# Moving window unpacking out of a ramp, dropping fillers, and cutting the last block's products into five pieces, in a graph attention kernel

## The chip, the cores and the metric

The kernel runs on one core of a Trainium2 chip. The metric is device time in microseconds (us). The profile's span, from the first to the last instruction, is about 1.8 us shorter than the time of the same run (289.9 against 291.72 for the kernel before). A 2% difference is 5.8 us.

PE is the matmul engine (TensorE) and PEld its weight load, DVE is VectorE, ACT is ScalarE, POOL is GpSimd, SP is SyncE, whose queue issues most transfers. L493 means line 493 of the kernel in question; the change shifts lines after 540 by a few.

## The reference

It is a graph attention layer on 4096 nodes with 64 features, 4 heads of 64, and 50,000 random edges:

```python
x_proj[h] = x @ weight[h]
score[h, e] = leaky_relu(x_proj[h, src] . att_src[h] + x_proj[h, dst] . att_dst[h], 0.2)
output[h, dst] += exp(score[h, e]) * x_proj[h, src]          # over all edges e
output[h, dst] /= sum of exp(score[h, e]) over edges into dst, + 1e-8
# result: 4096 x 256, f32
```

## The kernel before

It sorts the edges by destination (to about 112 us). Then it works on 33 blocks of 125 destination nodes; a block's edges are 16 tiles of 128. For each block the SP queue loads a table `bc` of 1 MB (edge keys, repeated on all partitions). VectorE turns it into one-hot matrices `oh`, TensorE gathers features and scores with them, ScalarE makes exponentials `ex` and copies `xs`, VectorE picks the leaky maximum (`wv`) and multiplies (`val`), and TensorE sums `val` into destinations and projects.

The tables come from `gat_bins` in HBM, which is filled by five "unpacks". Each serves eight blocks: window `i` serves blocks 8i to 8i+7.

```python
def unpack(self, i):                                   # Windows
    t, tb = self.t[:, i], self.tb[:, i]
    V.tensor_scalar(out=t[:, 1, :], in0=self.win[:, i, :], ..., op0=OP.bitwise_and)          # L441
    V.tensor_scalar(out=t[:, 0, :], in0=self.win[:, i, :], ..., op0=OP.logical_shift_right)  # L442
    e = G if i else V
    e.tensor_copy(out=tb[:, 1, :], in_=t[:, 1, :])                                           # L445
    e.tensor_scalar(out=tb[:, 0, :], in0=t[:, 0, :], scalar1=boff[:, i:i + 1], ...)          # L446
    nc.sync.dma_start(out=bin_dram[8 * i:8 * i + 8]..., in_=tb)                              # L447
```

`G` is GpSimd, `V` VectorE, `S` ScalarE, `T` TensorE. The `dma_start` on `nc.sync` goes into the same queue as the table loads and the results, and the traces show that queue in the program's order (before: bins at 126.06, block 5's load at 131.75, the first result at 137.60). The ramp, which fills the pipeline for blocks 0 to 2:

```python
busy(11)                       # fillers: matmuls without use, meant to keep TensorE's clock up
win.unpack(0)
for b in range(2, 5):
    blocks.load(b)
blocks.weights(0)
blocks.values(0)               # block 0's product
for c in range(len(CH)):       # block 1's table: made by TensorE ("spread", L479), copied by ScalarE (L481)
    blocks.spread(1, c, ...)
    if c == 1:
        blocks.onehot(1, *CH[0])
... # one-hots of block 1, sums of block 0, gathers of block 1
for i in range(1, NI):         # NI = 5
    win.unpack(i)
blocks.sums(0, 1)
busy(3)
blocks.onehot(2)
blocks.weights(1)
blocks.run(1)
```

And the loop:

```python
def run(self, first=0):
    for b in range(first, ND):
        self.load(b + 4)                               # 1 MB on the SP queue
        self.values(b, 2 if b == ND - 1 else 1)        # the product val
        self.gather(b + 1, 0); self.sink.project(b - 1); self.sums(b, -1)
        self.gather(b + 1, 1); self.gather(b + 1, 2)
        self.sink.invert(b - 1)
        self.onehot(b + 2, halves=(0,))
        self.weights(b + 1)
        self.onehot(b + 2, halves=(1,))
        self.sink.give(b - 1)                          # result, written on the SP queue
        self.sums(b, 0); self.sums(b, 1)
```

(Conditions on `b` and the line breaks are cut.)

## Time and profile before

| | before |
|---|---|
| time, median of 5 | 291.72 us (291.0 to 292.1) |
| span of the profiled run, mean granted clock | 289.9 us, 0.864 |
| busy share PE / DVE / ACT / POOL | 71 / 89 / 66 / 12 % |
| product `val` of blocks 1, 2, 3, 4 starts at | 131.40, 137.50, 142.82, 147.53 us |
| a block step from there on | 4.71 us |
| product of block 31 | 274.79 us |

A block's product occurs once a step, and in the loop the distance between two of them is 4.71 us. Whatever a version gains or loses can be read as a shift of this series, and located between two blocks. Time minus block 31's product is 16.93 us before.

### The profile page before, as it was taken

To read this page: it belongs to the slowest core of one execution; us is meant where nothing else is said; L and a number is where in the kernel's file an instruction comes from. 1 tells how busy PE (TensorE), PEld (TensorE's weight loads), DVE (VectorE), ACT (ScalarE), POOL (GpSimd) and SP (SyncE) were. 2 spreads that over 40 slices of the span, in tenths; PEclk is the share of its full clock that TensorE was granted. 3 is DMA by queue.
4 is the path that set the end of the run, shared out by engine and by line. 5 is a ranking of instruction groups with operands and counts; after the bars stand their busy time and mean duration, and the time that the engine had idled before them with its cause. 6 is when DMAs were issued, how large, how long until landed. Compare 5 with 4: busy or idle time off the path is not lost.

```text
span 289.9 us, 8530 instructions
## 1 busy us (share of the span) xinstructions
PE 205.4 (71%) x3531; PEld 195.1 (67%) x3531; DVE 259.3 (89%) x526; ACT 190.9 (66%) x392; POOL 33.9 (12%) x81
## 2 busy tenths in 40 slices
PE   0011899950000066859999999999999999999990
PEld 0010699950000025549999999999999999999980
DVE  5999999993699999857999999999999999999970
ACT  2960710041699938554888888888888888888860
POOL 7882000002000001751000000000000000000000
PEclk9999975555555559996999999999999999999997
DMA  3026000001100001495576766768586767675011
GB/s 110 0 55 111 0 2 0 0 2 40 33 0 0 0 0 40 174 331 170 202 278 225 276 242 255 263 232 288 211 295 214 293 217 283 224 267 190 23 38 43
DMA packets 12688, 40.77 MB, mean 141 GB/s; under 512 B 1840, under 2 KB 8272, under 8 KB 8672
## 3 DMA queue, kind: packets, MB, share of 16 engines
q1 hardware_dynamic: 10128, 37.91, 35.7%
q10 hardware_dynamic: 1808, 1.56, 2.3%
q0 software_dynamic: 704, 0.66, 1.2%
q8 instruction: 30, 0.49, 0.7%
q14 instruction: 18, 0.15, 0.2%
HBM read 35.08 MB, written 5.05 MB: 138 GB/s over the span
## 4 chain that ended last, share of the span: by engine, by line

## 5 line engine op out<-in xcount | busy, mean ns | idle before, releaser
L524 ACT CAST xs<-ps 128x1200 bf16<-128x1200 f32 (+1 forms) x99 | 104.1, 1052 | 0.0
L542 DVE TENSOR_TENSOR val<-xs,wv 128x4096 bf16<-128x4096 bf16 (+1 forms) x34 | 75.4, 2219 | 0.4 <-ACT xs L524 0.2
L516 PE MATMUL ps<-adb,oh 128*128 128x136 bf16 x528 | 62.7, 225 | 0.0
L514 PE MATMUL ps<-xa,oh 128*128 128x72 bf16 x528 | 59.9, 198 | 3.7 <-DVE oh L493 2.1
L567 PE MATMUL acc<-xs,val 128*128 128x125 bf16 x1024 | 62.0, 219 | 0.0
L567 PEld LDWEIGHTS <-val 128*128 128x128 bf16 x1056 | 58.8, 98 | 0.3 <-DVE val L542 0.3
L516 PEld LDWEIGHTS <-oh 128*128 128x128 bf16 x528 | 49.8, 99 | 1.5 <-issue 1.4
L514 PEld LDWEIGHTS <-oh 128*128 128x128 bf16 x528 | 47.6, 99 | 3.2 <-DVE oh L493 3.2
L281 PE MATMUL cnt_ps<-sgn,sel 128*128 128x17 f32 (+1 forms) x6 | 1.6, 385 | 60.7 <-ACT sgn L273 41.7
L493 DVE TENSOR_SCALAR oh<-bc,pF 128x4096 bf16<-128x4096 bf16 (+2 forms) x37 | 42.6, 1152 | 0.6 <-ACT bc L481 0.6
L281 PEld LDWEIGHTS cnt_ps<-sgn,sel 128*128 128x128 f32 x6 | 1.4, 318 | 60.8 <-issue 60.8
L522 ACT ACTIVATE ex<-ps 128x96 bf16<-128x96 f32 (+1 forms) x99 | 25.0, 252 | 26.2 <-PE ps L520 26.1
L202 DVE TENSOR_TENSOR sA<-sB 128x256 f32<-128x256 f32 (+2 forms) x104 | 37.2, 399 | 1.5
L202 DVE TENSOR_TENSOR sB<-sA 128x256 f32<-128x256 f32 (+2 forms) x98 | 35.1, 399 | 1.3
L520 PE MATMUL ps<-xa,oh 128*128 128x72 bf16 x528 | 33.9, 199 | 0.0
L520 PEld LDWEIGHTS <-oh 128*128 128x128 bf16 x528 | 26.9, 100 | 0.0
L495 DVE TENSOR_SCALAR oh<-bc,pF 128x2048 bf16<-128x2048 bf16 (+2 forms) x37 | 25.6, 691 | 0.0
L420 PEld LDWEIGHTS at_ps<-uv,xT 64*128 64x128 f32 x130 | 24.9, 298 | 0.3 <-issue 0.3
L420 PE MATMUL at_ps<-uv,xT 64*128 64x4 f32 x130 | 25.0, 329 | 0.0
L270 ACT ACTIVATE junk<-kr,nb 128x512 f32<-128x512 f32 x33 | 23.8, 722 | 1.1
L629 PE MATMUL pf<-Wbd,aT 128*128 128x128 f32 (+1 forms) x132 | 23.3, 299 | 0.5 <-ACT aT L621 0.5
L560 PEld LDWEIGHTS <-xs 128*128 128x128 bf16 x528 | 18.7, 96 | 0.4
(141 smaller groups left out, 231.0 us busy)
## 6 DMA issues: line engine op xcount, KB each, us to landing
bc<-gat_bins SPq DMA_DIRECT2D x31, 1024.0 KB, 5.1
out_dram<-res SPq DMA_DIRECT2D x32, 125.0 KB
eD<-in_edge_index_dram ACTq DMA_DIRECT2D x2, 195.0 KB, 3.3
eS<-in_edge_index_dram SPq DMA_DIRECT2D x2, 195.0 KB
gat_bins<-tb SPq DMA_DIRECT2D x5, 64.0 KB, 5.1
gat_sorted<-sA SPq DMA_DIRECT2D x1, 256.0 KB, 2.0
gat_sorted<-ki SPq DMA_DIRECT2D x1, 256.0 KB
win<-gat_sorted,to POOLq DMA_INDIRECT x5, 2.5
```

The source lines that it names most:

```text
L202: V.tensor_tensor(out=av(d[:], o, [2 * h, n], [1, h]), in0=av(s[:], 0, [2 * h, n], [1, h]), in1=av(s[:], h, [2 * h, n], [1, h]), op=op)
L270: S.activation(out=junk[:], in_=v, func=ACTF.Sign, bias=nbnd[:, b:b + 1], scale=1.0, accum_out=sgn[:, b:b + 1])
L420: T.matmul(out=ps[:, b, :], lhsT=xT[:, b * step:b * step + P], rhs=uv[:, k, :], start=(b == 0), stop=True, skip_group_check=True)
L493: V.tensor_scalar(out=oh[:, e], in0=bc[:, e], scalar1=pF[:, 0:1], scalar2=None, op0=OP.is_equal)
L495: V.tensor_scalar(out=av(oh[:], (2 * NT + t0) * W2, [W2, nt], [1, W2]), in0=av(bc[:], (2 * t0 + 1) * W2, [2 * W2, nt], [1, W2]), scalar1=p ...
L514: T.matmul(out=ps[:, i, P:P + XC], lhsT=hot(2 * t + 1), rhs=xa[:, 2 * t, :], start=(i % 2 == 0), stop=False, skip_group_check=True)
L516: T.matmul(out=ps[:, i, 0:S0], lhsT=hot(2 * t), rhs=adb[:, b, :], start=False, stop=False, skip_group_check=True)
L520: T.matmul(out=ps[:, i, P:P + XC], lhsT=hot(2 * NT + t), rhs=xa[:, 2 * t + 1, :], start=False, stop=True, skip_group_check=True)
L522: S.activation(out=av(ex[:], 2 * t0, [2, n], [2 * NT, 2 * H], [1, 2]), in_=av(ps[:], P, [PW, n], [1, 2 * H], [0, 2]), func=ACTF.Exp)
L524: S.copy(out=xs[:, t0:t0 + n, 0:P + XC], in_=ps[:, 0:n, 0:P + XC])
L542: V.tensor_tensor(out=av(val[:], h * Dout, [Dout, n], [C, NT], [1, Din]), in0=av(xs[:], S0, [0, n], [XW, NT], [1, Din]), in1=av(wv[:], h * ...
L567: T.matmul(out=self.to[k], lhsT=val[:, t, k * P:(k + 1) * P], rhs=xs[:, t, 0:self.n], start=apart and t == 0, stop=(t == NT - 1), skip_gro ...
```

## The change

Unpacks 3 and 4 serve blocks 24 to 32, yet VectorE waits for their windows in the ramp. The change moves them to the ends of block steps 1 and 2, drops seven of the ramp's fourteen fillers, and cuts the last block's product so that the second sum of the tail can begin earlier.

```diff
-            for h in range(0, H, n):
-                V.tensor_tensor(out=av(val[:], h * Dout, [Dout, n], [C, NT], [1, Din]), ...)
+            for h, nh, t, n in ((0, 2, 0, NT), (2, 1, 0, 12), (3, 1, 0, 12), (2, 1, 12, 4),
+                                (3, 1, 12, 4)) if parts > 1 else ((0, H, 0, NT),):
+                V.tensor_tensor(out=av(val[:], h * Dout + t * C, [Dout, nh], [C, n], [1, Din]), ...)
...
-        def run(self, first=0):
+        def run(self, first=0, also={}):
...
                 self.sums(b, 0)
                 self.sums(b, 1)
+                if b in also:
+                    also[b]()
...
-            if n != H:
-                m = min(n, 2 * BD)
-                S.copy(out=self.aT[b][:, at:at + m], in_=acc[:, 0:m])
+            elif n != H:
+                part = self.fp.tile([P, n], F32, name=f"part{at}")
+                S.copy(out=part[:], in_=acc)
...
-        busy(11)
+        busy(7)
...
-        for i in range(1, NI):
+        for i in range(1, 3):
             win.unpack(i)
         blocks.sums(0, 1)
-        busy(3)
         blocks.onehot(2)
         blocks.weights(1)
-        blocks.run(1)
+        blocks.run(1, {i - 2: lambda i=i: win.unpack(i) for i in range(3, NI)})
```

(The rest of the diff is bookkeeping for the part tiles.)

More of the change, by code (lines that the diff above doesn't have):

```diff
@@ L539, in values @@
             val = self.bp.tile([P, NT, C], BF16, name="val")
-            n = H // parts
-            for h in range(0, H, n):
-                V.tensor_tensor(out=av(val[:], h * Dout, [Dout, n], [C, NT], [1, Din]),
-                                in0=av(xs[:], S0, [0, n], [XW, NT], [1, Din]),
-                                in1=av(wv[:], h * 2 * NT, [2, n * NT], [0, Din // 2], [1, 2]), op=OP.mult)
+            for h, nh, t, n in ((0, 2, 0, NT), (2, 1, 0, 12), (3, 1, 0, 12), (2, 1, 12, 4),
+                                (3, 1, 12, 4)) if parts > 1 else ((0, H, 0, NT),):
+                V.tensor_tensor(out=av(val[:], h * Dout + t * C, [Dout, nh], [C, n], [1, Din]),
+                                in0=av(xs[:], S0 + t * XW, [0, nh], [XW, n], [1, Din]),
+                                in1=av(wv[:], h * 2 * NT + 2 * t, [2, nh * n], [0, Din // 2], [1, 2]), op=OP.mult)
             self.val[b] = val
@@ L610, in __init__ @@
             self.apart = True
-            self.aT = {}
+            self.aT, self.den = {}, {}
             self.fp = ctx.enter_context(tc.tile_pool(name="fin", bufs=2))
@@ L617, in take @@
             if n in (AW, H):
-                self.aT[b] = self.fp.tile([P, AW], F32, name="aT")
-            if n != H:
-                m = min(n, 2 * BD)
-                S.copy(out=self.aT[b][:, at:at + m], in_=acc[:, 0:m])
+                self.den[b] = self.fp.tile([P, AW], F32, name="aT")
+            t = self.den[b]
+            if n == AW:
+                S.copy(out=t[:, 0:2 * BD], in_=acc[:, 0:2 * BD])
+                self.aT[b] = [t[:, k * BD:k * BD + P] for k in range(2)]
+            elif n != H:
+                part = self.fp.tile([P, n], F32, name=f"part{at}")
+                S.copy(out=part[:], in_=acc)
+                self.aT.setdefault(b, []).append(part[:])
             if n in (AW, H):
-                S.activation(out=self.aT[b][:, 2 * BD:AW], in_=acc[:, n - H:n], func=ACTF.Identity, bias=eps[:, 0:1])
+                S.activation(out=t[:, 2 * BD:AW], in_=acc[:, n - H:n], func=ACTF.Identity, bias=eps[:, 0:1])
         def project(self, b):
             self.pf = self.psf.tile([P, C], F32, name="pf")
-            m = min(P, N - b * BD)
-            for k in range(2):
-                T.matmul(out=self.pf[0:m, k * P:(k + 1) * P], lhsT=self.aT[b][:, k * BD:k * BD + m], rhs=Wbd[:, k, :],
+            for k, t in enumerate(self.aT.pop(b)):
+                T.matmul(out=self.pf[0:t.shape[-1], k * P:(k + 1) * P], lhsT=t, rhs=Wbd[:, k, :],
                          start=(k == 0), stop=True, skip_group_check=True)
@@ L633, in invert @@
             self.inv = self.fp.tile([P, H], F32, name="inv")
-            V.reciprocal(out=self.inv[0:BD], in_=self.aT.pop(b)[0:BD, 2 * BD:AW])
+            V.reciprocal(out=self.inv[0:BD], in_=self.den.pop(b)[0:BD, 2 * BD:AW])
         def give(self, b, parts=1):
```

## The prediction

> **What bounds the kernel now.** I read the page first, then the table by stage, then VectorE's timeline at the two places that the change touches, and the waits there. The kernel is a sort (to about 112 us), a ramp that prepares the first blocks of 125 destination nodes (112 to 143 us), a steady loop over blocks (to 279 us) and a tail. The change touches the ramp and the tail. The table by stage (columns: stretch, its length, busy time of PE, PEld, DVE, ACT, POOL, then granted clock, DMA share, GB/s), cut at the points where the TensorE clock changes:
>
> ```profile
> 122.40:125.80 3.40, 3.40 (x76) 3.40 (x76) 2.88 (x9) 2.21 (x4) 1.09 (x3) 1.00 1.00 345
> 125.80:129.20 3.40, 1.24 (x11) 0.55 (x8) 0.83 (x5) 1.68 (x5) 2.11 (x6) 1.00 0.99 352
> 129.20:132.60 3.40, 2.16 (x21) 2.16 (x22) 3.30 (x4) 0.54 (x2) 2.10 (x2) 0.51 0.47 161
> 132.60:136.00 3.40, 3.40 (x53) 3.34 (x52) 2.35 (x3) 1.87 (x3) 0.00 (x0) 0.50 0.90 311
> 136.00:140.00 4.00, 4.00 (x87) 3.99 (x85) 3.64 (x6) 2.88 (x7) 0.00 (x0) 0.99 0.34 110
> 222.00:268.60 46.60, 46.60 (x995) 46.48 (x992) 46.31 (x60) 39.28 (x79) 0.00 (x0) 1.00 0.66 239
> ```
>
> In the loop (last line) PE and DVE are both full. From 125.8 to 129.2 both are nearly idle, and the two stretches after it run TensorE at half clock. What VectorE does there (start, duration, line, operation, and in brackets its idle time and who ended it):
>
> ```profile
> 125.06 0.21 DVE L442 TENSOR_SCALAR t<-win 128x128 int32<-128x128 int32 x1
> 127.00 0.23 DVE L441 TENSOR_SCALAR t<-win 128x128 int32<-128x128 int32 x1 [1.72 <-DMA win<-gat_sorted,to]
> 127.14 0.22 DVE L442 TENSOR_SCALAR t<-win 128x128 int32<-128x128 int32 x1
> 128.73 0.23 DVE L441 TENSOR_SCALAR t<-win 128x128 int32<-128x128 int32 x1 [1.37 <-DMA win<-gat_sorted,to]
> 128.87 0.22 DVE L442 TENSOR_SCALAR t<-win 128x128 int32<-128x128 int32 x1
> 129.00 1.38 DVE L493 TENSOR_SCALAR oh<-bc,pF 128x4096 bf16<-128x4096 bf16 x1
> 130.31 0.85 DVE L495 TENSOR_SCALAR oh<-bc,pF 128x2048 bf16<-128x2048 bf16 x1
> 131.08 0.21 DVE L534 TENSOR_TENSOR wv<-ex 128x128 bf16<-128x128 bf16 x1
> 131.40 2.29 DVE L542 TENSOR_TENSOR val<-xs,wv 128x4096 bf16<-128x4096 bf16 x1
> 133.61 0.17 DVE L634 RECIPROCAL inv<-aT 125x4 f32<-125x4 f32 x1
> 133.69 1.26 DVE L493 TENSOR_SCALAR oh<-bc,pF 128x4096 bf16<-128x4096 bf16 x1
> 136.36 0.22 DVE L534 TENSOR_TENSOR wv<-ex 128x128 bf16<-128x128 bf16 x1 [1.41 <-ACT ex L522]
> ```
>
> The reader is to see that VectorE stands in line behind window transfers 3 and 4 (1.72 and 1.37 us), which serve blocks 24 to 32 only, while block 2's one-hot matrix (129.00) waits behind them in program order. The 1.41 us at 136.36 is the echo: TensorE at half clock delivers block 2's gathers late. The next block has 0.64 us of the same, then the loop runs at 4.71 us a block (val at 147.53 for block 4 and 274.79 for block 31: 127.26 / 27 = 4.713).
>
> [...] the half-clock stretch is 129.24 to 136.07, 6.83 us[...]; in the one before it PE was busy 1.24 us, three fillers included, which did not save the clock. [...] POOL's step L446 takes 0.60 us when VectorE idles and 2.02 us at 129.28 beside the one-hots, which themselves take 1.38 and 0.85 instead of 1.25 and 0.75.
>
> **The change, part by part.** The order of instructions in the changed kernel confirms what moves.
>
> Fillers. Four of eleven matmuls are dropped at 116.2. They end at 118.6 (about 0.216 us each), and the spread matmuls of block 1 begin at 118.60, although their operand is written by 118.14. Without four, the spread begins at about 118.2, ScalarE's copy 0.4 us earlier, and VectorE's next one-hot, which waited 0.40 us for that copy at 120.97, starts at about 120.55 when the product before it ends. Gain: 0.4 us at most; I count 0.35[...]. The other three fillers (127.5) lie in the idle gap and cost and give nothing.
>
> Unpacking. Unpacks 1 and 2 stay; unpacks 3 and 4 move to the end of block steps 1 and 2. Each is two VectorE instructions of 0.13 us start to start, so 0.27 us each, moved and not saved; what goes is the waiting before them. Block 2's one-hot then starts at 125.2 - 0.4 = 124.8. Is its table there? In the DMA queue's packet records, the 128 packets for block 2 land by 124.0, those for block 3 by 128.5, for block 4 by 131.9. So yes, by 0.8 us. VectorE then goes on: one-hot 1.31 and 0.77, weights 0.32 start to start, so block 1's product starts at about 127.2 instead of 131.40. TensorE ends block 1's gathers and block 0's sums at about 125.9 and gets the first half one-hot at 126.1: the gap shrinks from over 4 us to a few tenths, and the clock stays full.
>
> From there VectorE has, start to start, product 2.20, reciprocal 0.09, one-hot 1.18, weights 0.14, half one-hot 0.66, result 0.34, and once in each of the first two steps 0.27 of unpacking: 4.88 us. So products of blocks 2 and 3 start at 132.1 and 137.0 instead of 137.50 and 142.82. TensorE at full clock needs 4.71 a block and fits. After block 3 the loop is as before. Block 3's table (128.5) is wanted at 129.5, block 4's (131.9) at 134.4.
>
> Against it stands POOL's share: eight POOL steps (four unpacks) now run beside VectorE instead of in its idle time. From 0.13 and 0.10 us measured on the two one-hots, I charge 0.3 us more.
>
> The same sum from the waits: VectorE's idle time that goes is 0.40 + 1.72 + 1.37 + 1.41 + 0.64 = 5.54 us; as start-to-start gaps (instructions overlap by about 0.08) it is 0.2 more, less the POOL charge of 0.3. Ramp: 5.4 us.
>
> Tail. The last block's product is in two halves of 2048 elements:
>
> ```profile
> 279.08 2.36 DVE L542 TENSOR_TENSOR val<-xs,wv 128x2048 bf16<-128x2048 bf16 x2 [0.16 <-ACT xs L524]
> 281.50 0.71 PEld L567 LDWEIGHTS <-val 128*128 128x128 bf16 x16 [0.26 <-DVE val L542]
> 281.62 0.42 DVE L642 TENSOR_TENSOR res<-pf,inv 125x256 f32<-125x256 f32 x1
> 282.68 0.24 PEld L629 LDWEIGHTS pf<-Wbd,aT 128*96 128x96 f32 x2 [0.28 <-ACT aT L621]
> ```
>
> From 2.28 us for 4096 elements and 2.36 for two of 2048 comes about 0.16 us fixed (0.08 of it overlapped) and 0.52 ns an element. Five pieces (2048, 768, 768, 256, 256) start at 279.08, 280.22, 280.70, 281.18, 281.39 and end at 281.68, 0.24 later than two. But TensorE's second sum needs only the first three to begin: 281.26 instead of 281.44. Its 0.26 us of waiting shrinks to 0.08, so the sum ends 0.18 earlier. The later end of the pieces pushes block 31's result (281.62) to 281.86, ending at 282.28, and the last projection overwrites its PSUM tile, so its first pair starts at 282.4 and its second at 282.62 instead of 282.68. Tail gain: 0.05 to 0.15, say 0.1. The head-pair copies in their own tiles remove no wait that I see: the first pair's projection already started (282.16) before the second copy (282.39).
>
> Sum: 5.4 + 0.1 = 5.5 us; 291.72 - 5.5 = 286.2.
>
> **The rivals.** First, a transfer takes the place of the wait. The SP queue issues in order, so the table load of block 5 follows the bins of unpack 2, that of block 6 the bins of unpack 3, that of block 7 those of unpack 4. If VectorE starves POOL, as at 129.28, bins 2 go out near 132 and block 5's table lands at 137; wanted at about 139.3. For blocks 6 and 7 I get landings near 142.3 and 146.7 against 143.8 and 148.5. Margins of 1.5 to 2 us speak against it; if POOL is slower still, 1 to 2 us come back: 287.5. Second, the clock falls anyway, because fewer fillers leave a window idle around 118 to 122; then TensorE runs 3.4 or 6.8 us at half rate and the old echo (about 2 us) returns: 288. The window 119.0 to 122.4 had PE busy some 2.1 us before and stayed warm, and keeps about that. Third, the gain is larger: in the loop, weights start at 273.65, just when the exponentials end (273.62), and one-hot to weights takes 1.28 where 1.18 would do, so TensorE with ScalarE sets the 4.71 and VectorE has 0.1 us of slack a block. If the unpacks and POOL contention hide in that, and TensorE alone counts, its chain starts up to 6.3 us earlier: 285.3. Against it, the first two steps are VectorE's.
>
> **Range and chances.** The central sum is 5.5, the optimistic 6.4, the pessimistic 4. Two per cent is 5.83 us, 285.89. The estimate stands just short of that: 286.2, range 285.2 to 287.5; faster by over 2% 0.34, within 2% 0.64, slower 0.02.
>
> **What would show it.** After: no VectorE idle time for windows near 125 us; block 2's one-hot near 124.8; clock 1.00 from about 109 to the end of the loop; products of blocks 1, 2, 3 near 127.2, 132.2, 137.2; loop pace unchanged at 4.71; the wait before the second sum of the last block under 0.1. Wrong would be: a one-hot waiting for a table load in blocks 3 to 7, half clock in the ramp, POOL steps that stretch VectorE's by over 0.3 us, or a tail that moves more than 0.3.

## More of the kernel before

The SP queue in the ramp (start, duration, queue, line, transfer, count):

```profile
119.88 1.27 SPq L469 DMA_DIRECT2D bc<-gat_bins  x3
126.06 5.59 SPq L447 DMA_DIRECT2D gat_bins<-tb  x4
131.75 0.38 SPq L469 DMA_DIRECT2D bc<-gat_bins  x1
137.99 0.33 SPq L469 DMA_DIRECT2D bc<-gat_bins  x1
143.27 0.32 SPq L469 DMA_DIRECT2D bc<-gat_bins  x1
147.98 0.32 SPq L469 DMA_DIRECT2D bc<-gat_bins  x1
```

The loads of blocks 5, 6, 7 and 8 go out about 5 us apart and nothing holds them.

POOL's two steps of one unpack, beside an idle VectorE:

```profile
126.00 0.28 POOL L445 CAST tb<-t 128x128 bf16<-128x128 int32 x1
126.26 0.60 POOL L446 TENSOR_SCALAR tb<-t,boff 128x128 bf16<-128x128 int32 x1
```

## The result

The changed kernel took 289.39 us, the median of five runs (288.37 to 289.64), against 291.72. The ratio is 0.9913, with a 95% interval of 0.9888 to 0.9939. Ratios here are the mean time of one kernel's fast runs over that of the other's fast runs of the same rounds, so not quite the ratio of the medians quoted. Executions over 1.5% slower than the fastest of the same kernel are left out of the means. The gain is 2.3 us of the 5.5 predicted, and even the fastest run lies outside the predicted range.

The profiled run was the fastest one (288.37 us, span 286.5, clock 0.873). Its stages, in the columns of the prediction's first table (the first two stretches are cut as a_again's clock windows lie, for the comparison below). A clock window is here a stretch of 3.41 us counted from the rise of the clock: the stretches in the clock records are multiples of it, 20.48 us full and 6.83 half in before and 174.08 full in after, which is 6, 2 and 51 times 3.413.

```profile
120.86:124.27 3.41, 2.44 (x51) 2.32 (x51) 2.81 (x5) 2.42 (x4) 1.73 (x2) 1.00 0.95 332
124.27:127.68 3.41, 3.20 (x66) 2.88 (x63) 3.41 (x10) 3.08 (x7) 2.42 (x2) 1.00 1.02 360
127.68:131.00 3.32, 3.32 (x71) 3.22 (x72) 3.22 (x4) 2.81 (x7) 3.32 (x3) 1.00 0.74 294
131.00:136.00 5.00, 4.96 (x106) 4.82 (x104) 5.00 (x9) 4.15 (x11) 3.81 (x3) 1.00 0.65 202
222.00:268.60 46.60, 46.60 (x992) 46.48 (x990) 46.27 (x60) 39.57 (x80) 0.00 (x0) 1.00 0.65 228
```

The idle stretch near 126 us and the half clock after it are gone. VectorE's order in the same place:

```profile
121.46 0.62 DVE L493 TENSOR_SCALAR oh<-bc,pF 128x1536 bf16<-128x1536 bf16 x1 [0.67 <-ACT bc L481]
...
125.38 0.22 DVE L442 TENSOR_SCALAR t<-win 128x128 int32<-128x128 int32 x1
125.51 1.31 DVE L493 TENSOR_SCALAR oh<-bc,pF 128x4096 bf16<-128x4096 bf16 x1
...
127.84 2.30 DVE L543 TENSOR_TENSOR val<-xs,wv 128x4096 bf16<-128x4096 bf16 x1
...
132.77 2.28 DVE L543 TENSOR_TENSOR val<-xs,wv 128x4096 bf16<-128x4096 bf16 x1
...
137.66 2.28 DVE L543 TENSOR_TENSOR val<-xs,wv 128x4096 bf16<-128x4096 bf16 x1
...
141.65 0.22 DVE L534 TENSOR_TENSOR wv<-ex 128x128 bf16<-128x128 bf16 x1 [0.45 <-ACT ex L522]
...
142.79 2.28 DVE L543 TENSOR_TENSOR val<-xs,wv 128x4096 bf16<-128x4096 bf16 x1
...
152.38 2.28 DVE L543 TENSOR_TENSOR val<-xs,wv 128x4096 bf16<-128x4096 bf16 x1
...
158.38 2.28 DVE L543 TENSOR_TENSOR val<-xs,wv 128x4096 bf16<-128x4096 bf16 x1
```

The counterpart of the first line in the kernel before:

```profile
120.97 0.80 DVE L493 TENSOR_SCALAR oh<-bc,pF 128x1536 bf16<-128x1536 bf16 x1 [0.40 <-ACT bc L481]
```

Block 2's one-hot (125.51) follows the unpacking without a wait. Products 1, 2 and 3 start at 127.84, 132.77 and 137.66, so block 3 is 5.16 us ahead of before, close to the 5.4 predicted for the ramp. Then time is given back. The step from block 3 to 4 takes 5.13 us, that from 5 to 6 takes 4.88, and that from 6 to 7 takes 6.00, where 4.71 is normal. From block 3 to block 7 that is 20.72 us instead of 18.85, so 1.87 us are lost. The remaining 3.30 are kept to block 31, and with 0.05 from the tail (16.93 less 16.88) they make the 3.35 us between the two profiled runs.

Where the largest loss is, TensorE stops between the two sums of a block (the columns as before; the bracket is idle time and what ended it):

```profile
152.27 1.04 PE L568 MATMUL acc<-xs,val 128*128 128x125 bf16 x16 [1.15 <-issue]
...
157.24 0.23 DVE L534 TENSOR_TENSOR wv<-ex 128x128 bf16<-128x128 bf16 x1 [1.32 <-ACT ex L522]
```

"issue" means that the profile shows nothing that TensorE waited for: its operands were there, since VectorE had ended the product by 149.78, the stop began at about 150.9, and the first of the block's two sums over it had run. VectorE's wait of 1.32 us, half a step later, is the echo. A second such stop, 138.33 to 139.03, precedes the 0.45 us at 141.65.

In the trace's packet records there is a queue of kind "instruction" with packets of 16 KB, 30 before and 29 after. From the second of them to the 28th TensorE starts 6649 instructions before and 6676 after, 256 and 257 a packet, so I take them to be TensorE's own. Numbering TensorE's instructions from the start (matmuls, weight loads and waits alike), the two stops come just before number 1217 and number 1729, that is 449 + 3 x 256 and 449 + 5 x 256. The packets concerned began only at 136.65 and 150.01 us, took 0.96 and 0.95, and TensorE resumed 1.4 and 1.3 us after each had ended. They began when TensorE was 69 and 34 instructions short of the place where it stopped; in the kernel before the same two packets began 272 and 124 short, and nothing stopped. So I read the stops as TensorE having run out of instructions: the place, the late packet and the lack of any other wait say so, and no record names it.

What was in the way is on the SP queue:

```profile
127.77 4.17 SPq L447 DMA_DIRECT2D gat_bins<-tb  x2
132.04 0.39 SPq L469 DMA_DIRECT2D bc<-gat_bins  x1
...
137.31 0.32 SPq L447 DMA_DIRECT2D gat_bins<-tb  x1
137.69 0.43 SPq L469 DMA_DIRECT2D bc<-gat_bins  x1
...
141.70 0.32 SPq L447 DMA_DIRECT2D gat_bins<-tb  x1
142.07 0.42 SPq L469 DMA_DIRECT2D bc<-gat_bins  x1
142.90 0.29 SPq L651 DMA_DIRECT2D out_dram<-res  x1
143.24 0.70 SPq L469 DMA_DIRECT2D bc<-gat_bins  x1
```

The load of block 6 (137.69) stands behind the bins of unpack 3 (137.31), that of block 7 (142.07) behind those of unpack 4 (141.70). Before, each load left about 0.45 us after a product started (block 7's at 143.27, product 3 at 142.82). Now block 7's leaves 4.41 us after product 3, nearly a whole step late, while block 8's is in time (0.45 after product 4). So these two leave 1.2 us apart where 4.7 was the rule, 2 MB at once, with the instruction packet of 150.01 in their wake. (The earlier packet, of 136.65, began before block 6's load left. Of the loads, only that of block 5 was under way then, 132.04 to 137.20, so two at once are seen for the larger stop only.) The bins are late because POOL is slow:

```profile
125.74 2.01 POOL L446 TENSOR_SCALAR tb<-t,boff 128x128 bf16<-128x128 int32 x1
...
127.97 3.62 POOL L446 TENSOR_SCALAR tb<-t,boff 128x128 bf16<-128x128 int32 x1
132.78 2.42 POOL L445 CAST tb<-t 128x128 bf16<-128x128 int32 x1 [1.19 <-DVE t L441]
135.18 2.11 POOL L446 TENSOR_SCALAR tb<-t,boff 128x128 bf16<-128x128 int32 x1
```

An unpack takes POOL 2.42 + 2.11 = 4.5 us beside a working VectorE, against 0.28 + 0.60 before, beside an idle one. Where the prediction had only L446 slow (2.02 us at 129.28), both steps of an unpack are slowed now.

The tail went as predicted, in VectorE's and TensorE's rows:

```profile
275.79 2.56 DVE L543 TENSOR_TENSOR val<-xs,wv 128x2048 bf16<-128x2048 bf16 x5 [0.16 <-ACT xs L524]
277.23 1.49 PEld L568 LDWEIGHTS <-val 128*128 128x128 bf16 x32
```

The two sums now follow one another as 32 weight loads without the wait of 0.26 between them. From the first piece to the issue of the last output is 4.51 us, against 4.62 before.

### The profile page after: what moved, and what is told of

Its sections match the earlier page's. It is cut to its first block, busy times and chain, and to the rows that moved or that the text cites. A ratio compares the mean times of both kernels' runs of the same rounds, so it can differ in the third digit from the quotient of the medians.

```text
span 286.5 us, 8520 instructions
## 1 busy us (share of the span) xinstructions
PE 202.4 (71%) x3524; PEld 192.9 (67%) x3524; DVE 259.0 (90%) x529; ACT 190.8 (67%) x392; POOL 44.0 (15%) x81
## 4 chain that ended last, share of the span: by engine, by line
## 5 line engine op out<-in xcount | busy, mean ns | idle before, releaser
L543 DVE TENSOR_TENSOR val<-xs,wv 128x4096 bf16<-128x4096 bf16 (+3 forms) x37 | 75.6, 2051 | 0.4 <-ACT xs L524 0.2
L516 PE MATMUL ps<-adb,oh 128*128 128x136 bf16 x528 | 61.3, 223 | 0.0
L514 PE MATMUL ps<-xa,oh 128*128 128x72 bf16 x528 | 58.8, 196 | 1.7 <-ACT bc L481 1.1
L516 PEld LDWEIGHTS <-oh 128*128 128x128 bf16 x528 | 49.0, 98 | 1.5 <-issue 1.4
L514 PEld LDWEIGHTS <-oh 128*128 128x128 bf16 x528 | 47.0, 98 | 1.0 <-DVE oh L493 0.9
L520 PE MATMUL ps<-xa,oh 128*128 128x72 bf16 x528 | 33.3, 197 | 0.1
L520 PEld LDWEIGHTS <-oh 128*128 128x128 bf16 x528 | 26.3, 99 | 0.2 <-DVE oh L495 0.2
L420 PEld LDWEIGHTS at_ps<-uv,xT 64*128 64x128 f32 x130 | 26.0, 311 | 0.2 <-issue 0.2
L420 PE MATMUL at_ps<-uv,xT 64*128 64x4 f32 x130 | 26.1, 338 | 0.0
L636 PE MATMUL pf<-Wbd,aT 128*128 128x128 f32 x128 | 21.9, 294 | 0.5 <-ACT aT L624 0.5
```

The source lines that it names most:

```text
L420: T.matmul(out=ps[:, b, :], lhsT=xT[:, b * step:b * step + P], rhs=uv[:, k, :], start=(b == 0), stop=True, skip_group_check=True)
L514: T.matmul(out=ps[:, i, P:P + XC], lhsT=hot(2 * t + 1), rhs=xa[:, 2 * t, :], start=(i % 2 == 0), stop=False, skip_group_check=True)
L516: T.matmul(out=ps[:, i, 0:S0], lhsT=hot(2 * t), rhs=adb[:, b, :], start=False, stop=False, skip_group_check=True)
L520: T.matmul(out=ps[:, i, P:P + XC], lhsT=hot(2 * NT + t), rhs=xa[:, 2 * t + 1, :], start=False, stop=True, skip_group_check=True)
L543: V.tensor_tensor(out=av(val[:], h * Dout + t * C, [Dout, nh], [C, n], [1, Din]), in0=av(xs[:], S0 + t * XW, [0, nh], [XW, n], [1, Din]), ...
```

## The experiments

Twelve kernels ran, in four groups, each group on one chip with its own runs of the kernel before. The letters in the expectations stand for the theories they were set against: T, loads that go out bunched delay TensorE's instruction packets, so that it stops; Q, the wider form, that bins held the SP queue, so that a loss follows block 3 in one way or the other; P, POOL's unpacking itself slows the engines, wherever its bins go; R, TensorE falls to half clock in the ramp; C, the same, as a matter of how idle TensorE is at 119 to 124 us; F, seven fillers are too few; S, the removed wait was a cushion which hid lateness in front of it.

For every profile the same sum works, within 0.35 us: time = start of product 3, plus what is lost from block 3 to 7 against four steps of 4.71, plus 148.8 us. That gives 291.6 for before (291.72 measured), 288.3 for after (288.37) and 290.3 for the first experiment (290.37). So this table of the profiled runs says where each stands:

| run | full clock from | half clock after that, us | product 0 | product 1 | product 3 | lost to block 7 | profiled run, us |
|---|---|---|---|---|---|---|---|
| before | 108.8 | 6.8 from 129 | 118.27 | 131.40 | 142.82 | 0.0 | 291.72 |
| after | 107.7 | none | 118.49 | 127.84 | 137.66 | 1.9 | 288.37 |
| a_again | 107.2 | 3.4 from 124 | 118.64 | 130.52 | 140.49 | 1.0 | 290.37 |
| b_tail_only | 109.1 | 6.8 from 130 | 118.56 | 132.06 | 143.32 | 0.0 | 291.99 |
| c_fillers_back | 107.9 | none | 118.64 | 128.05 | 139.26 | 1.1 | 288.89 |
| d_bins_pool_queue | 113.0 | none | 120.14 | 130.00 | 139.81 | -0.1 | 288.55 |
| e_load_first | 107.4 | 3.4 from 114, 3.4 from 124 | 118.97 | 130.76 | 140.73 | -0.1 | 289.80 |
| h_11_fillers | 113.5 | 3.4 from 124 | 120.17 | 130.77 | 140.75 | 0.9 | 290.40 |
| g_queue_and_11 | 113.6 | 3.4 from 124 | 120.07 | 130.78 | 140.78 | -0.1 | 289.22 |
| x_extra_load | 109.3 | 6.8 from 130 | 118.50 | 131.41 | 143.09 | 0.0 | 292.97 |
| k_before_plus10 | 108.0 | none | 118.45 | 131.64 | 141.00 | 0.0 | 290.06 |
| l_load_first_plus10 | 108.5 | none | 119.06 | 129.67 | 139.49 | 0.2 | 288.19 |
| j_gap_fillers | 107.3 | none | 118.58 | 127.33 | 137.15 | -0.1 | 285.71 |
| m_gap_only | 117.1 | none | 121.90 | 130.56 | 140.38 | 0.0 | 289.19 |

(x_extra_load has another 0.84 us from the loads added to it.) The second column belongs to the end of the sort, which no kernel here changes: the clock rises there between 107 and 109.5 in ten profiles, at 113 to 114 in three and at 117 in one; in those four block 0's product starts 1.6 to 3.4 us late. In those four block 0's spread still runs at half clock: its matmuls start 0.21 us apart, and 0.11 in the others. That is a difference between executions, and it has to be kept apart from what a version does.

### a_again: the changed kernel once more

No edit. It asks whether one profile of the changed kernel is typical.

> The changed kernel once more, unaltered. Its five runs so far fall in two groups, 288.4 to 288.7 and 289.4 to 289.6 us. Theory T (TensorE waits for its own instructions: two gaps of 0.70 and 1.37 us, both at a place 449 + a multiple of 256 in its instruction stream, each ending 1.3 us after a 16 KB packet of the instruction queue that came late behind the table loads): the gaps are there again at the same places in the stream, with other lengths, and a slower profile has longer gaps or one more. Rival R (a stretch at half clock in the ramp makes the slower group): the slower profile shows granted clock 0.5 between 120 and 145 us and no longer gaps. Ratio 0.991 either way.

Measured: 289.91 us (288.7 to 290.42, 4 runs), ratio 0.9956 (0.9905 to 1.0008). The same kernel has another profile. PE was busy for only 1.11 us of one clock window, and the next ran at half clock:

```profile
120.86:124.27 3.41, 1.11 (x23) 0.99 (x23) 1.54 (x4) 2.78 (x2) 0.89 (x1) 1.00 0.98 365
124.27:127.68 3.41, 3.41 (x41) 3.41 (x40) 3.41 (x10) 1.30 (x2) 1.08 (x2) 0.50 1.00 271
```

The cause of the idleness was a late spread. VectorE waited 1.87 us at 122.80 for ScalarE's copy of block 1's table, and the half clock then made block 1's exponentials and copies late, another 0.85 and 0.49 us. Product 1 started at 130.52. Later there was no stop for instructions at the packet boundary. Instead the table itself was late:

```profile
153.33 1.29 DVE L493 TENSOR_SCALAR oh<-bc,pF 128x4096 bf16<-128x4096 bf16 x1 [1.13 <-DMA bc<-gat_bins]
```

Here the step from block 5 to 6 took 5.84 us. So a held SP queue shows in either of two ways, as a one-hot without its table (1.13 us here) or as a stop of TensorE at a packet boundary (1.37 us in after). The stops that T expected at the same places didn't come, so T as written for this run failed and its wider form Q is what is left. And the clock of the ramp is a second, separate loss, which differs from run to run: R holds for this profile.

### b_tail_only: the tail parts on the kernel before

```diff
+ (the five pieces, part tiles)          - (all ramp edits: 11 and 3 fillers, four unpacks in the ramp)
```

> Only the tail of the change (last block's product in five pieces, copies in own tiles), the ramp as before. By my sum 0.05 to 0.15 us faster, ratio 0.9995; from the first piece of the last product to the issue of the last output transfer 4.5 us instead of 4.62. If the tail carries more of the measured 2.3 us than I think, the ratio is under 0.998.

Measured: 290.74 us (290.58 to 291.99, 4), ratio 0.9997 (0.9952 to 1.0041). The tail alone moves nothing that these runs can see, which is no surprise for 0.1 us. From the first piece to the issue of the last output it takes 4.52 us, as expected. The ramp of this run is that of before, half clock from 129.58 to 136.41.

### c_fillers_back: the change with its fillers back

```diff
-        busy(7)
+        busy(11)
...
         blocks.sums(0, 1)
+        busy(3)
         blocks.onehot(2)
```

> The change, but with all 11 and 3 filler matmuls as before; only the unpacking moves (and the tail). My prediction had the fillers cost 0.35 us, so this would be 0.35 us slower than the changed kernel. The changed kernel's trace says otherwise: its copy of block 1's first tables starts 1.49 us after the spread matmuls where it was 0.90 before. If the fillers do nothing for the end, the two are equal within 0.2 us. Theory T: TensorE's gaps stay, because nothing about the loads changes. A rival to T, that the gaps come from where the shorter program puts its instructions, has them gone or moved in time.

Measured: 291.33 us over all four, one of which was slow; the three fast ones are 288.89, 290.85 and 291.81, ratio 1.0044 (0.9983 to 1.0106). With the window waits gone the three late fillers are not free:

```profile
128.22 0.81 PE L722 MATMUL warm<-adb,identb 128*128 128x512 bf16 x3 [1.29 <-ACT aT L631]
```

They write the sums' accumulator, so they must wait until ScalarE has read block 0 out of it, 1.29 us, and block 1's gathers stand behind them. The step from block 1 to 2 took 6.31 us instead of 4.93. The prediction's "cost and give nothing" was true of the kernel before only; dropping them is a necessary part of the change. The table wait came as in a_again (1.21 us), without a stop for instructions.

### d_bins_pool_queue: the bins leave on another queue

```diff
-            nc.sync.dma_start(out=bin_dram[8 * i:8 * i + 8]..., in_=tb)
+            (nc.gpsimd if i else nc.sync).dma_start(out=bin_dram[8 * i:8 * i + 8]..., in_=tb)
```

> The change, but the bins of unpacks 1 to 4 are written from GpSimd's own queue, so that the SP queue no longer holds the table loads of blocks 5, 6 and 7 until GpSimd has unpacked. Theory T with bunched loads as the reason for late instruction packets: loads of blocks 5 to 8 go out some 5 us apart instead of at 132.0, 137.7, 142.1, 143.2; the 1.37 us gap near 151 us goes, the 0.70 us gap near 138.7 goes or stays; 1 to 2 us faster than the changed kernel, some 287.4 to 288.4. Rival: [...] the table loads were no cause: equal or slower, with the gap still there.

Measured: 287.56 us (286.17 to 289.69, 4), ratio 0.9886 (0.9812 to 0.996). The loads now leave when their turn comes. The first line holds the loads of blocks 2 to 5 together:

```profile
121.66 5.95 SPq L469 DMA_DIRECT2D bc<-gat_bins  x4
...
135.13 0.33 SPq L469 DMA_DIRECT2D bc<-gat_bins  x1
...
139.97 0.32 SPq L469 DMA_DIRECT2D bc<-gat_bins  x1
...
144.92 0.32 SPq L469 DMA_DIRECT2D bc<-gat_bins  x1
```

The steps from block 3 on are 4.62, 4.71, 4.72 and 4.71, with neither a table wait nor a stop for instructions. Q holds for the loss after block 3. In this execution the clock rose only at 113, product 0 started at 120.14 instead of 118.49, and the whole ramp is that much later, so its time in the table shows nothing of the gain; its two best runs, 286.17 and 286.57, do.

### e_load_first: the table load goes ahead of the bins

Unpacks 3 and 4 are called just after the next step's table load, so that the load isn't behind their bins.

```diff
                 self.load(b + 4)
+                if b - 1 in also:
+                    also[b - 1]()
                 self.values(b, 2 if b == ND - 1 else 1)
...
-                if b in also:
-                    also[b]()
```

> The change, but unpacks 3 and 4 are called just after the next step's table load and not before it: VectorE's order is the same, the SP queue issues the load of blocks 6 and 7 before the bins that wait for GpSimd. Theory Q (the SP queue, held by bins that wait for GpSimd's 4.5 us of unpacking, sends the loads of blocks 6 to 8 late and bunched; the loss shows as a one-hot that waits for its table, 1.1 to 1.2 us in two profiles, or as TensorE waiting for instructions that come late behind bunched loads): the steps from block 3 on take 4.7 us each, no wait for a table; some 1.2 us faster than the changed kernel (289.4), so 288.2. Rival P (GpSimd's unpacking itself slows the engines, wherever its bins go): the loss stays, 289.4. A third outcome is possible under Q: loads 5 and 6 now go out together near 132, and TensorE's instruction packet of that time comes late: a gap at 449 + 3*256 in its stream.

Measured: 288.03 us (286.35 to 289.8, 6), ratio 0.9891 (0.9835 to 0.9947). No loss after block 3, as expected, by another route than in d, and with POOL's unpacking as slow as ever (2.42 + 2.10 us), so P falls. But the six runs fall into two groups: 286.35, 286.35 and 287.0 with mean granted clocks of 0.875 to 0.881, and 289.05, 289.33 and 289.8 with 0.858 to 0.864. A window of 3.41 us at half clock is worth 3.41 x 0.5 / 287 = 0.006 of the mean clock. The profiled run belongs to the second group. It has PE busy 1.10 us in the window from 121.08, half clock from 124.50 to 127.92, product 1 at 130.76, and another such window before its ramp. With the transfers mended, the faster group is where the prediction had put the kernel, and the slower one fits half clock in one window or two.

### h_11_fillers and g_queue_and_11: are seven fillers too few?

```diff
-        busy(7)
+        busy(11)          # h: the changed kernel; g: together with d's queue
```

> The change with the eleven fillers of before at 116 us, and still without the three at 127 us. In three profiles with seven fillers ScalarE's copy of block 1's tables began 1.49, 2.10 and 2.78 us after the first spread matmul; in three with eleven 0.90, 0.90 and about 1.07. Theory F (seven fillers are too few there, TensorE is late with the spread): the copy begins about 0.9 to 1.1 us after the spread, block 1's product starts at 127.6 or before, and the kernel is 0.3 to 1 us faster than the changed one. My prediction's step says the reverse, 0.35 us slower. Loss behind block 3 unchanged.

> Both remedies together: bins on GpSimd's queue and eleven fillers at 116 us, none at 127. If theories Q and F both hold, nothing of the predicted ramp gain is lost: block 1's product near 127.5, steps of 4.9, 4.9, then 4.7 us, no wait for a table, clock full; 286.0 to 287.0, ratio 0.982 to 0.985, which was my prediction for the change itself. If only Q holds, as the run with GpSimd's queue alone (287.6).

Measured for h: 289.2 us (287.53 to 292.45, 6, one slow), ratio 0.9921 (0.9873 to 0.9968). For g: 288.78 (286.12 to 291.2, 6, one slow), ratio 0.9889 (0.9829 to 0.9949). Both profiles show a half-clock window from 124 all the same, after one in which PE was busy 1.26 and 1.23 us. Product 1 started at 130.77 and 130.78; 1.6 us of its lateness comes from the clock at 113, the rest from this window and the late spread before it. Against after (289.39) and d (287.56) there is no difference that would be clear. F falls: four more fillers at this place don't save the clock. The pair also repeats Q: h lost 0.9 us after block 3 and g nothing. In the times of single versions this hardly shows, as their intervals overlap. Pooled, the nine fast runs of a_again and h (loads held) have a mean of 289.25 us, the fifteen of d, e and g (not held) one of 287.89, all on one chip: 1.4 us, with a 95% interval of about 1 either way.

### x_extra_load: two more loads in the middle of the kernel before

To see whether traffic alone can starve TensorE of instructions, two loads of 1 MB into a tile that nobody reads were added after those issued in steps 13 and 14, far from any ramp or unpack.

```diff
                 self.bc[b] = t
+                if self.sink.apart and b in (17, 18):
+                    nc.sync.dma_start(out=spare[:], in_=...bin_dram[b]...)
```

(The added line stands just before `self.bc[b] = t` in the kernel.)

> The kernel before with two transfers more: the table loads of blocks 17 and 18 (issued some 20 us ahead of their use) are each followed by a copy of the same 1 MB into a tile that nobody reads. No engine waits for them. Theory T (bunched loads delay TensorE's instruction packets): one or two 16 KB packets of the instruction queue come late near 190 to 205 us, TensorE has a gap of 0.3 us or more at 449 + a multiple of 256 (here 463, as 14 instructions stand before), where the trace shows no wait, and the time rises by as much. Rival: instruction packets are not hurt by load traffic, or the tables are what is late: no such gap; at most a one-hot waits for the tables of blocks 18 to 20, by under 1 us.

Measured: 292.11 us (291.19 to 292.97, 4), ratio 1.0035 (0.9987 to 1.0083). The profile:

```profile
204.03 0.45 PEld L570 LDWEIGHTS <-val 128*128 128x128 bf16 x8 [0.67 <-issue]
204.03 0.61 PE L570 MATMUL acc<-xs,val 128*128 128x125 bf16 x8 [0.50 <-issue]
```

The sum stops after 24 of 32 matmuls, from 203.32 to 204.03. That is before TensorE's instruction 3777 = 449 + 13 x 256, again a packet boundary. The packet began at 201.69, took 0.95 us, and came 440 instructions after the one ahead of it, where the same packet came 355 after it in the kernel before; TensorE resumed 1.39 us after its end. The steps to blocks 17 and 18 took 5.36 and 4.90 us, 0.84 in all above 4.71. The boundary that I had expected was off by 14 instructions (I had counted from a wrong start), but no unpack and no ramp is near, and the kernel before has no such stop there: in this profile the packet came late beside the bunched loads, and TensorE stopped for 0.71 us at its boundary. The time itself moves less than its interval.

### k_before_plus10 and l_load_first_plus10: was the wait a cushion?

Ten more fillers at 116 us, once in the kernel before and once in e. They hold the spread back on purpose.

```diff
-        busy(11)
+        busy(21)          # k, on before
-        busy(7)
+        busy(17)          # l, on e_load_first
```

> The kernel before with 21 fillers instead of 11 at 116 us: TensorE reaches block 1's spread matmuls ten times 0.216 us = 2.2 us later. Theory S (before, the wait for windows 3 and 4, whose transfers end at fixed times near 127 and 128.7 us, swallows any lateness of TensorE ahead of it; the change took that cushion away, so that lateness now counts in full): VectorE's idle time before the two window instructions shrinks by about 2 us, block 2's one-hot still starts near 129.0 to 129.6, time within 0.4 us of before. Rival (TensorE's chain sets block 2's start in both kernels): 2 us slower, 293.

> The changed kernel in its load-first form (288.03, ratio 0.9891) with ten fillers more at 116 us (17 instead of 7). Theory S: no cushion, so it is 1.5 to 2.2 us slower than the load-first form: 289.5 to 290.2, ratio 0.995 to 0.998. If more fillers keep TensorE's clock full in the ramp (in four of seven profiles of changed kernels it fell to half at about 124 us for 3.4 us, in those block 1's product started at 130.5 to 130.8), part of that comes back: 289. Rival to S: no slower than the load-first form.

Measured for k: 290.25 us (289.83 to 291.27, 6), ratio 0.9969 (0.9943 to 0.9995). Its VectorE:

```profile
123.55 0.62 DVE L493 TENSOR_SCALAR oh<-bc,pF 128x1536 bf16<-128x1536 bf16 x1 [2.80 <-ACT bc L481]
...
129.06 0.32 DVE L441 TENSOR_SCALAR t<-win 128x128 int32<-128x128 int32 x1 [1.10 <-DMA win<-gat_sorted,to]
```

The one-hot of block 1 waited 2.80 us instead of 0.40, but the windows still came at the same time, so the wait for them shrank from 1.72 + 1.37 to 1.10, and product 1 started at 131.64 instead of 131.40: 2.4 us of lateness cost 0.24. In the kernel before, the window wait was a cushion under everything ahead of it. (That k is faster than before by 1 us was not expected. In its profile the clock stays full, and the step from block 1 to 2 is 4.64 us and not 6.10.)

Measured for l: 288.14 us (287.47 to 289.04, 6), ratio 0.9892 (0.9866 to 0.9918), full clock. By the time alone the forecast missed: l is no slower than e (288.03), which was the outcome named against S. But e's median mixes runs with and without half clock, and it ran on another chip. The profile of l shows the lateness going through: no window wait absorbs it, and product 1 starts at 129.67, which is 2.34 us later than in j below, on the same chip; the time is 1.7 us longer. As j also has five fillers at another place, that pair is not a clean one. For the kernel before, k shows the cushion; that lateness counts in full without it is seen in l's profile and not proved by its time. (l also stops for 0.33 us before instruction 1729, a packet boundary, though the loads around it left 4.5 to 4.9 us apart; the load of block 8 took 8.7 us to land.)

### j_gap_fillers: fillers where the idle time is

The idle stretch in a_again lies after block 1's first two spread parts, while TensorE waits 2.79 us for ScalarE to free the next buffer. So five fillers go there, on top of e.

```diff
             if c == 1:
                 blocks.onehot(1, *CH[0])
+                busy(5)
```

> The load-first form with five more fillers in the place where TensorE idles 1.2 to 3 us in the ramp, behind the spread matmuls of block 1's first two parts, while it waits for ScalarE's copies. Theory C (part of the lost ramp gain is the half-clock stretch at 124 us, which depends on how idle TensorE is between 119 and 124): profile without clock 0.5 between 110 and 280 us, block 1's product at 128 to 129, median 286.5 to 287.2, and less spread between runs than 286.35 to 289.8. If the fillers only get in the way: 288.5 or more, with the same spread.

Measured: 286.47 us (285.71 to 286.8, 6), ratio 0.9833 (0.9809 to 0.9858). The windows:

```profile
117.50:120.91 3.41, 3.27 (x22) 1.90 (x21) 3.23 (x8) 1.44 (x2) 3.10 (x2) 1.00 0.23 58
120.91:124.32 3.41, 3.07 (x65) 2.90 (x63) 3.37 (x7) 2.42 (x4) 1.72 (x2) 1.00 0.96 344
124.32:127.74 3.42, 3.21 (x62) 2.89 (x60) 3.32 (x9) 2.99 (x9) 2.99 (x4) 1.00 1.01 350
```

All are full and PE is busy over 3 us in each. The products start where the prediction had them:

```profile
127.33 2.30 DVE L543 TENSOR_TENSOR val<-xs,wv 128x4096 bf16<-128x4096 bf16 x1
...
132.26 2.28 DVE L543 TENSOR_TENSOR val<-xs,wv 128x4096 bf16<-128x4096 bf16 x1
...
137.15 2.28 DVE L543 TENSOR_TENSOR val<-xs,wv 128x4096 bf16<-128x4096 bf16 x1
```

No step after them exceeds 4.72. The times lie within 1.1 us, where those of e took up 3.5. That is not all the fillers' doing, or not shown to be: e ran on another chip, l without them on j's chip took up 1.6, and m with them on a third took up 2.9. This version beats both kernels: it is 4.8 us below the before of its rounds (291.23), and 2.9 below the median of the changed kernel, though not in the same rounds.

### m_gap_only: the gap fillers without the reordering

```diff
             if c == 1:
                 blocks.onehot(1, *CH[0])
+                busy(5)           # on the changed kernel: bins still ahead of the loads
```

> The changed kernel with the five gap fillers alone, the table loads still held behind the bins. With load-first and gap fillers together it was 286.47 (ratio 0.9833); this run sizes the two parts. Theory Q: with the clock full and all earlier, the loss behind block 3 is there in full, 1.0 to 1.3 us: about 287.6, ratio 0.987; in the profile block 1's product near 127.4, clock full through the ramp, and behind block 3 either a one-hot that waits about 1 us for a table or a TensorE gap at 449 + a multiple of 256 (459 here, as ten instructions stand before). If clock and cushion were all and the held loads nothing: 286.5, equal to the run with both.

Measured: 288.06 us (286.3 to 289.24, 6), ratio 0.9898 (0.9859 to 0.9937). Against j that is 1.6 us longer, which fits a loss of 1 to 1.9 after block 3, but on another chip, and the profile doesn't show it. In this execution the clock rose only at 117.06, so product 0 started at 121.90 instead of 118.58. The gap fillers did their part: no window fell afterwards, and product 1 came 8.66 us after product 0, as in j (8.75), where after took 9.35 and a_again 11.88. And from block 3 to 7 next to nothing was lost (steps 4.63, 4.76, 4.80, 4.71). So m's profile owes its length to the late rise. Its queue was held all the same: the load of block 7 left 4.91 us after product 3 and 0.87 before that of block 8, just as in h. But it landed 6.85 us later, as VectorE came to its one-hot, where in h it took 7.73 and cost 1.03 us. Held loads, then, cost time in most executions and not in every one: four of five profiles with held loads lost 0.9 to 1.9 us, and d, e, g, l and j, where nothing held them, at most 0.2. Whether the held loads or the late rise account for the rest of m's runs stays open.

## Why the prediction was wrong

What was right. The mechanism is as predicted: unpacks 3 and 4 had held VectorE at the windows, and the half clock after it was the echo. Both go. Block steps 1 and 2 took 4.93 and 4.89 us against the 4.88 worked out. The loop keeps 4.71. The 0.3 us charged for POOL's effect on VectorE were too much, as those two steps exceed the sum by 0.06 together. The tail gained 0.1. And j, which repairs what follows, has its products at the predicted places and its median 0.3 us from the predicted time. So the sum of the parts was a fair picture of a ramp in which nothing else goes wrong.

What was wrong are three steps which had kept 286.2 free of losses.

**The first rival's margins.** "Margins of 1.5 to 2 us speak against it." The loads left about when the prediction must have had them. It has 5 us from block 5's bins to its table (132 to 137); by the same 5 us the landings at 142.3 and 146.7 mean that blocks 6 and 7 leave at 137.3 and 141.7, and they left at 137.69 and 142.07 in the profile of after. The mis-sized term is the landing. With block 8's load 0.9 us behind it, block 7's took 7.84 us in a_again, 7.91 in c and 7.73 in h, 2.7 to 2.9 more than those 5, which is more than the margin; the one-hot waited 1.0 to 1.2 us. In the profile of after it took 5.99 and was 1.7 us ahead of its one-hot, so there the margin held, and the 1.9 us went by a path that the prediction did not have: TensorE stopping, as I read it, for its own instructions (0.70 and 1.37 us), which x_extra_load produced without the change (0.71 us). The loss is gone in d, e, g and j, which take the loads out from behind the bins in two different ways. Its size, 1 to 2 us, is the rival's own. "After block 3 the loop is as before" is the step that failed here.

**The second rival.** "The window 119.0 to 122.4 had PE busy some 2.1 us before and stayed warm, and keeps about that." Counted in windows of 3.41 us from the rise at 107.72, the profile of after has 1.86 and 2.96 us there (117.97 to 124.79) and stays at full clock. Not so a_again (1.11), e (1.10), h (1.26) and g (1.23): each of these four has half clock in the window after it. From product 0 to 1 they take 10.6 to 11.9 us, where after takes 9.35 and j 8.75. The rise that the windows are counted from lies between 107.2 and 117.1 us, and the spread's lateness varies from 0.89 to 2.77, so one before-profile that stayed warm said little. The prediction had 288 for this rival alone; e's slower runs are at 289 to 290. The reason given there, fewer fillers, was not the right one: h and g have the old eleven and lose the window as well. With fillers at the place of the idleness no window fell in the profiles of j or m, nor in that of l with ten more at the old place (all at clock 1.00 from the rise on), which cost time (l is 1.7 us behind j). The later rise of the clock at the end of the sort, in four of the profiles, was not thought of at all.

**The fillers' gain of 0.35 us.** It was to come from an earlier spread. In after the one-hot waits 0.67 us for ScalarE's copy, longer than the 0.40 before, and product 1 starts at 127.84, 0.6 later than predicted. The spread began at 118.50 instead of 118.2, and its first part was done late. Behind this is a thing that the prediction did not consider: lateness ahead of the window wait had cost next to nothing, as k shows, so the profile before could not tell whether that part of the ramp was in time. With the cushion away nothing absorbs it (l).

For the profiled run of after, the miss of 2.2 us is 1.9 for the held loads and 0.3 for the later ramp (the sum above puts block 3 at 286.2 - 148.8 = 137.4 against 137.66). For a_again the miss of 4.2 us is 1.0 for the loads and 3.1 for the ramp with its half clock. The other runs of after have no profile; their mean clocks, 0.866 to 0.872 against 0.873, suggest that some had a half-clock window more, which is argued and not shown.

What stays open. The spread's completion lags by an amount that varies. From its first matmul to the start of ScalarE's copy it is 0.90 us before and 0.89 to 0.90 in k, l, j and m, but 1.49 in after, 2.77 in a_again, 2.69 in e, and 2.10 to 2.16 in d, g and h. A TensorE at half rate is not the reason. By its semaphore in the trace, it reports the first two parts done 0.66 us apart in before, k, l, j and m, 0.73 and 0.76 apart in a_again and e, and 0.08 apart in after, d, h and g; at recorded half clock (block 0's spread in d, h, g and m) they are 1.28 apart. So the reports come late as a whole, or the first does, at full rate, and what delays them is not known. Why the clock rises at 107, 113 or 117 was not tested. The 3.41 us windows, counted from the rise, lie differently against the fillers at the end of the sort in each execution, but busy time alone does not order them: a window with PE busy 2.73 us was followed by full clock in x_extra_load, and two with 2.84 and 2.87 in m were not. It does not order those after the rise either: windows with 1.10, 1.11, 1.23 and 1.26 us busy (e, a_again, g, h) were followed by half clock, and so was one with 1.78 (e, from 110.85), while those with 1.47 (d, from 119.86), 1.79 (a_again, from 110.61) and 1.86 (after, from 117.97) were not. Nor was it tested whether j escapes the late rise: none of its six times looks like such a run. And the shares of queue and clock in the median can't be split exactly, since each profile is one draw and the groups of runs were on different chips.

## What to carry to other kernels

Before removing a wait, ask what it hides: everything that ends ahead of it may have had free slack, so the profile before can't tell whether that was in time, and a run with deliberate lateness there can (k costs one edit). A margin against a transfer needs its slow landings and not one: 5 us had been allowed, and in the profile of after tables took 5.1 to 8.8. When work moves into a full loop, follow it to the queue it ends in: here 64 KB of bins, waiting for 4.5 us of POOL's unpacking, held a load of 1 MB until 4.41 us after product 3, where it left 0.45 us after it in the kernel before; with the load issued first (e) nothing was lost there. Put fillers where the engine is idle, not where they are convenient: five in the idle stretch took the profile of j to product 1 at 127.33, seventeen at the old place that of l to 129.67. And judge a clock by several executions: after had no half clock in the ramp, and the same kernel had 3.41 us of it in a_again.
